# The first modulation computed by pairs of feature tiles, with five strips in flight and unused products between them

## The chip, the cores and the metric

The kernel runs on one core of one Trainium2 chip. TensorE (PE, with its weight load PEld) multiplies; VectorE (DVE) and ScalarE (ACT) do the elementwise work; GpSimd (POOL) does little here; SyncE (SP) issues the DMAs. The metric is the device time of one execution in microseconds (us). Lower is better.

## The reference, cut to what matters

Two blocks run one after the other. The change lies in the opening of layer 0 of the first one. With x of 256 tokens by 1024 features and a conditioning vector c:

```python
mod = silu(c) @ w_ada + b_ada
shift, scale, gate = split(mod, 3, axis=-1)
h = rmsnorm(x, norm_g) * (1.0 + scale) + shift
proj = h @ w_in
...
xbc = silu(causal_dwconv(xbc, conv_w, conv_b))
...
dt = softplus(dt_raw + dt_bias)
```

The 3072 columns of `mod` are 1024 of shift, 1024 of scale and 1024 of gate. Nothing of `proj` can be complete before all 1024 features of h are modulated, so before all of shift and scale are known. Rotary tables (sine and cosine of the positions) are used further on, by the retention heads.

## The kernel before

**Layout.** Features lie on partitions, as eight tiles of 128 features by 256 tokens; x is one buffer of 1 MB. A column block of 128 of `w_in` is a *strip*: its weights come as one 0.5 MB transfer `raw` (L491), ACT copies them, rounded, into `hi` (through the helper at L479), DVE writes the remainder `lo = raw - hi` (L506), and PE multiplies (`mm3`, L533 to L535) with three products for each feature tile: hi by h_hi, hi by h_lo, lo by h_hi. A strip is 8 x 3 = 24 products of 128x128 by 128x256 into one accumulator bank. `hi` and `lo` have three buffers each; strip 3 is one of a few named in `EXTRA` and uses two other buffers (`ret_o`, `fox_v`). The strips come in a fixed list; the first nine are four of the convolution's B and C part, one for dt and the gates' inputs, and then four of the convolution's xs part.

**The modulation.** `mod` comes in rounds of 512 columns. A round is 4 raw tiles of 0.5 MB, loaded as two transfers of 1 MB into two of four buffers (`yd`, `qk_ret`, `xs`, `xdt`, which other steps use later), so that two rounds are in flight. PE multiplies each half of a round in 16 small products with 32 columns of silu(c) (L718, on the trace 32 records, since each is two passes), ACT copies the sums (`ada_0s` to `ada_3s`), PE transposes them (L725) and DVE adds the bias (`mod`). Rounds 0 and 1 are the shift, rounds 2 and 3 the scale; `first_norm` takes them in the order 0, 2, 1, 3. After 0 and 2 feature tiles 0 to 3 of h can be made, after 1 and 3 tiles 4 to 7: for each tile ACT writes `h_hi`, DVE the modulated value (L472) and `h_lo` (L457).

**The norm.** Beside that ACT and DVE square and add x (`sq`, `acc`), PE sums over partitions (L635), DVE makes the reciprocal root in small steps (`rs13y`), PE spreads it over partitions (L644) and DVE multiplies x by it (`qk_fox`). Then come 8 products of 128x128 that spread silu(c) (`spread`, L783), whose results are used by the later rounds on VectorE.

**The strips behind it.** Strips 0, 1 and 2 start with what tiles 0 to 3 give; `BEHIND` holds their first products behind products of rounds 1 and 3. Each finished strip of B and C goes through `conv4`: ACT writes `cv_y` from the bank, DVE adds three shifted taps (`cv_y`, 255, 254 and 253 wide), ACT makes `cv_t`, DVE multiplies into `BC`. Strip 4 goes through `dtf` (`dtf_z`, the softplus `sp`, running sums). Banks of tag `mm` are three; the third tap frees one. Between them stand DVE's 16 steps and ACT's two lookups for the rotary tables (`rot_ang`, `rot_n`, `rot_r`, `rsin`, `rcos`; L831).

**Order.** Instructions on an engine run in the order that a scheduler gives them by priorities and by `issue_after` edges; an engine waits at the head of its queue.

## Time and profile before

| | us |
|---|---|
| median of 3 runs | 2198.2 |
| lowest, highest | 2197.14, 2200.11 |
| profiled execution, its own time | 2200.12 |
| its span, first to last instruction | 2198.4 |
| PE busy in the span | 2146.0 (98%) |
| DVE busy in the span | 1714.4 (78%) |
| ACT busy in the span | 1000.6 (46%) |

All the rest of the document reads one profiled execution. A row of the timeline gives the start of an instruction (or of a run of like ones, x n), its duration, what it is, output from inputs with partitions and elements, and in brackets how long the engine had been idle before it and what it then had waited for. A row of the windows gives for a stretch the busy time of each engine with its instruction count. Durations of neighbours overlap by about 0.1 us, since an engine starts the next before the last has drained; where costs are added, the distance between two starts is used.

### The profile page before, as it was taken

Reading aid. Unit: us, or ns where it says so; the run is one execution under the profiler, and the core shown is the slowest. Engines: PE = TensorE matmul, PEld = TensorE weight load, DVE = VectorE, ACT = ScalarE, POOL = GpSimd, SP = SyncE. Lnnn points to the kernel's source line nnn. Section 1 sums busy time; section 2 is a strip of 40 time slices with the busy share of each in tenths; the row PEclk is TensorE's granted clock in tenths of the full one; section 3 lists DMA queues with packets and bytes.
Section 4 is the critical chain, followed back from the end, with each engine's and each line's share of the span. In section 5 each row is a group of like instructions: output and inputs, shape, how many; then the busy total and the mean of one; then the engine's idle time right before and its main releaser. Section 6 shows DMA issues by size and latency. Waiting matters only on the chain. (4 is left out here: it accounts for less than half of the span.)

```text
span 2198.4 us, 38207 instructions
## 1 busy us (share of the span) xinstructions
PE 2146.0 (98%) x14481; PEld 1910.5 (87%) x14481; DVE 1714.4 (78%) x3551; ACT 1000.6 (46%) x1828; POOL 72.0 (3%) x657
## 2 busy tenths in 40 slices
PE   6999999999999999999999999999999999999999
PEld 5999989898877888888888888888887999999999
DVE  6986889798975999775476777766689977567877
ACT  4656555555455333432333443323355434445654
POOL 0000000001000000000000000000000000000000
PEclk9999999999999999999999999999999999999999
DMA  8665746567321144235443244453432453674665
GB/s 301 198 202 176 268 135 201 160 215 235 106 68 53 50 128 144 82 123 160 125 154 110 82 125 128 122 181 122 122 116 72 128 156 126 210 249 145 186 195 158
DMA packets 98264, 330.71 MB, mean 150 GB/s; under 512 B 10912, under 2 KB 14368, under 8 KB 97952
## 3 DMA queue, kind: packets, MB, share of 16 engines
q1 hardware_dynamic: 97632, 326.47, 47.0%
q8 instruction: 114, 1.87, 0.4%
q0 software_dynamic: 448, 1.81, 0.2%
q14 instruction: 70, 0.57, 0.1%
HBM read 325.08 MB, written 3.15 MB: 149 GB/s over the span
## 5 line engine op out<-in xcount | busy, mean ns | idle before, releaser
L479 ACT ACTIVATE hi<-raw 128x1024 fp32r<-128x1024 f32 (+3 forms) x494 | 492.0, 997 | 709.0 <-PE mm L534 440.0
L506 DVE TENSOR_TENSOR lo<-raw,hi 128x1024 fp32r<-128x1024 f32 (+3 forms) x494 | 565.0, 1144 | 231.0 <-ACT hi L479 228.3
L533 PE MATMUL mm<-h,hi 128*128 128x512 f32 (+1 forms) x1296 | 445.7, 345 | 3.4 <-ACT th L479 1.2
L535 PE MATMUL mm<-h,lo 128*128 128x512 f32 (+1 forms) x1296 | 442.0, 342 | 2.5 <-DVE lo L506 2.5
L534 PE MATMUL mm<-h,hi 128*128 128x512 f32 (+1 forms) x1296 | 442.1, 342 | 0.4 <-DVE h L475 0.4
L533 PEld LDWEIGHTS mm<-h,hi 128*128 128x128 f32 x1296 | 244.3, 189 | 33.7 <-ACT h L479 1.5
L535 PEld LDWEIGHTS mm<-h,lo 128*128 128x128 f32 x1296 | 244.8, 189 | 32.3 <-DVE lo L506 3.3
L534 PEld LDWEIGHTS mm<-h,hi 128*128 128x128 f32 x1296 | 244.7, 189 | 30.3 <-DVE h L475 0.8
L533 PE MATMUL mm<-hi,h 128*128 128x256 f32 x608 | 173.2, 285 | 0.8 <-ACT h L479 0.7
L534 PE MATMUL mm<-lo,h 128*128 128x256 f32 x608 | 171.8, 283 | 1.2 <-DVE lo L506 1.2
L535 PE MATMUL mm<-hi,h 128*128 128x256 f32 x608 | 172.2, 283 | 0.1
L533 PE MATMUL mm<-h_hi,hi 128*128 128x256 f32 x512 | 143.7, 282 | 4.0 <-ACT h_hi L479 2.3
L535 PE MATMUL mm<-h_hi,lo 128*128 128x256 f32 x512 | 143.4, 282 | 1.3 <-DVE lo L506 1.2
L534 PE MATMUL mm<-h_lo,hi 128*128 128x256 f32 x512 | 143.8, 282 | 0.7 <-DVE h_lo L457 0.5
L475 DVE SCALAR_TENSOR_TENSOR cv<-glu,vec,cv 128x512 f32<-128x512 f32 (+1 forms) x240 | 136.4, 615 | 2.5 <-ACT cv L479 2.4
L766 DVE SCALAR_TENSOR_TENSOR ada<-ada,cb 128x1024 f32<-128x1024 f32 x104 | 126.8, 1220 | 1.3 <-DMA ada<-aall 0.8
L533 PEld LDWEIGHTS mm<-hi,h 128*128 128x128 f32 x608 | 114.4, 188 | 2.7 <-ACT h L479 1.8
L534 PEld LDWEIGHTS mm<-lo,h 128*128 128x128 f32 x608 | 114.5, 188 | 2.1 <-DVE lo L506 1.4
L535 PEld LDWEIGHTS mm<-hi,h 128*128 128x128 f32 x608 | 114.6, 189 | 1.3 <-DVE h L475 0.9
L533 PEld LDWEIGHTS mm<-h_hi,hi 128*128 128x128 f32 x512 | 96.1, 188 | 5.1 <-ACT h_hi L479 2.7
L535 PEld LDWEIGHTS mm<-h_hi,lo 128*128 128x128 f32 x512 | 96.1, 188 | 2.1 <-DVE lo L506 1.9
L534 PEld LDWEIGHTS mm<-h_lo,hi 128*128 128x128 f32 x512 | 96.3, 188 | 1.6 <-DVE h_lo L457 1.1
(679 smaller groups left out, 4821.9 us busy)
## 6 DMA issues: line engine op xcount, KB each, us to landing
raw<-wall SPq DMA_DIRECT2D x400, 512.0 KB, 3.7
ada<-aall SPq DMA_DIRECT2D x120, 512.0 KB, 4.2
raw<-wall SPq DMA_DIRECT2D x32, 384.0 KB, 3.1
raw<-wall SPq DMA_DIRECT2D x32, 320.0 KB, 3.1
raw<-wall SPq DMA_DIRECT2D x32, 256.0 KB, 2.7
yd<-aall SPq DMA_DIRECT2D x2, 1024.0 KB, 10.3
qk_ret<-aall SPq DMA_DIRECT2D x2, 1024.0 KB, 11.3
xs<-aall SPq DMA_DIRECT2D x2, 1024.0 KB, 10.8
```

Of the source, the lines that this page charges most:

```text
L475: return self.nc.vector.scalar_tensor_tensor(out=out, in0=a, scalar=s, in1=b, op0=op0, op1=op1)
L479: return self.nc.scalar.activation(out, a, f, bias=bias, scale=scale, **kw)
L506: self.last_lo = self.nc.vector.tensor_tensor(lo[:, :w], raw[:, :w], hi[:, :w].bitcast(F32), op=ALU.subtract)
L533: mm(ps, ah, bh, start=first and n == 0, stop=False)
L534: mm(ps, ah, bl, start=False, stop=False)
L535: self.last_mm = mm(ps, al, bh, start=False, stop=last and n == len(A) - 1)
L766: nc.vector.scalar_tensor_tensor(out=out, in0=raw, scalar=1.0, in1=self.cb[which][i], op0=ALU.mult, op1=ALU.mult, accum_out=m[:, n:n + 1])
```

## The change

The rounds 0 to 3 are cut otherwise: round r now holds the 256 columns of shift and the 256 of scale of feature tiles 2r and 2r+1, so each round completes one pair of tiles. x and the second group of vectors are loaded ahead of the first round's weights. Five strips (`FIRST_STRIPS`) advance with the rounds: after round 1 all five multiply tiles 0 to 3 (60 products), after round 2 three of them tiles 4 and 5 (18), after round 3 the two others (`OWED`) catch up on tiles 4 and 5 (12) and all five take tiles 6 and 7 (30). Strip 4 also gets buffers of its own (`fox_k`, `fox_o`, its raw tile under the tag `ada`), and two strips use banks of the tag `aux`. `idle` adds products of the identity by itself, which nothing reads: 20 ahead of round 0's first half, and then after each first half, after each second half and after each transpose the numbers in `IDLE`, 69 in all. The `spread` moves from the norm to behind the third strip's first part. The constants' second group (801 KB), the fox mask, the small dt vector and the rotary tables are held behind the split of strip 6 or later, the tables with a low priority (`ROT_LATE`).

```diff
@@ -31,7 +31,7 @@
...
 ADA_STRIPS = [a + d * i for a, d, n in ADA_AT for i in range(n)]
-EXTRA = (3, 72, 244, 423)
+EXTRA = (3, 4, 72, 244, 423)
 FIRST_TAGS = ("yd", "qk_ret", "xs", "xdt")
@@ -49,8 +49,12 @@
...
 ZFIRST = 4
-SPREAD = 0
-BEHIND = ((1, 3), (3, 3), (3, 3))
+FIRST_STRIPS = 5
+IDLE = ((20, 4, 6), (6, 2, 10), (4, 2, 8), (1, 2, 1, 3))
+OWED = 3
+ROT_LATE = 260
 ADA_LATE = 300
@@ -172,18 +176,20 @@
-FIRST_ROUNDS = (0, 2, 1, 3)
+def _mixed(which, l, r):
+    return (which, l) == (1, 0) and r < 4
 def _ada_plan():
...
         for l in range(2):
-            order = FIRST_ROUNDS + (4, 5) if (name, l) == ("w_ada", 0) else range(rounds)
-            for r in order:
+            which = 1 if name == "w_ada" else 2
+            for r in range(rounds):
                 for q in range(4):
-                    if (1 if name == "w_ada" else 2, l, r) in ON_PE:
-                        s.append((name, l, _full(2, 256 * q), ((512 * r, 512),)))
+                    if (which, l, r) in ON_PE:
+                        cols = ((256 * r, 256), (1024 + 256 * r, 256)) if _mixed(which, l, r) else ((512 * r, 512),)
+                        s.append((name, l, _full(2, 256 * q), cols))
                     else:
@@ -487,10 +492,13 @@
...
         nm = f"{self.wpos}"
-        raw = self.wp.tile([P, 1024], F32, tag="raw", name="raw" + nm, bufs=RAW_BUFS)
+        early = self.wpos in EXTRA and self.wpos < FIRST_STRIPS
+        tag, bufs = ("ada", 2) if early else ("raw", RAW_BUFS)
+        raw = self.wp.tile([P, 1024], F32, tag=tag, name="raw" + nm, bufs=bufs)
         self.nc.sync.dma_start(out=raw[:, :w], in_=self.wall[self.woff:self.woff + P * w].rearrange("(p w) -> p w", p=P))
         if self.wpos in EXTRA and self.wpos < N_PLAN1:
-            hi, lo = [self.bt([P, 1024], tag, FR, 1) for tag in ("ret_o", "fox_v")]
+            tags = ("fox_k", "fox_o") if self.wpos == 4 else ("ret_o", "fox_v")
+            hi, lo = [self.bt([P, 1024], tag, FR, 1) for tag in tags]
         elif self.wpos in EXTRA:
@@ -570,6 +578,12 @@
...
         return self.last_ada
+    def idle(self, n):
+        for _ in range(n):
+            mm = self.nc.tensor.matmul(self.scrap[:, :P], self.ident, self.ident, start=True, stop=True)
+        return mm
     def warm(self, behind, act, n):
@@ -587,12 +601,11 @@
...
             self.bg.popleft()()
-    def proj_f(self, name, act, T0, T, behind=None):
+    def proj_f(self, name, act, T0, T):
         w = self.strip(name)
         ps = self.mm_bank()
-        with self.tc.issue_after(behind.ins) if behind else nullcontext():
-            self.mm3(ps[:, :T], w, [(a[:, T0:T0 + T], b[:, T0:T0 + T]) for a, b in act])
+        self.mm3(ps[:, :T], w, [(a[:, T0:T0 + T], b[:, T0:T0 + T]) for a, b in act])
         return ps[:, :T]
@@ -717,17 +730,26 @@
...
                                           start=k == 0, stop=k == 7)
-            self.round_mm[which, l, r, q] = mm
+            if idle and q == 1:
+                with self.tc.issue_after(mm.ins):
+                    mm = idle(0)
+        if idle:
+            with self.tc.issue_after(mm.ins):
+                mm = idle(1)
         self.last_ada = mm
...
         pt = self.ps("tr")
-        nc.tensor.transpose(pt[:, :P], s, self.ident)
+        self.last_tr = nc.tensor.transpose(pt[:, :P], s, self.ident)
         def finish():
...
                 col = 0 if which == 1 else 1 + i
-                self.add(m[:, 4 * r:4 * r + 4], pt[:, col:P:32], b)
+                if _mixed(which, l, r):
+                    two = lambda a: a[:, 0:16].rearrange("p (a k) -> p a k", a=2)[:, :, 2 * r:2 * r + 2]
+                    self.add(two(m), pt[:, 0:P:32].rearrange("p (a k) -> p a k", a=2), two(self.v("b_ada0")))
+                else:
+                    self.add(m[:, 4 * r:4 * r + 4], pt[:, col:P:32], b)
         if later:
@@ -884,19 +906,18 @@
...
         if l == 0:
-            self.first_norm(rb, h)
+            first = self.first_norm(rb, h)
         else:
+            first = []
             mod = self.mods[1, l][0]
...
         for n in range(4):
-            behind = self.round_mm[(1, 0) + BEHIND[n]] if l == 0 and n < len(BEHIND) else None
-            self.conv4(l, self.proj_f("w_in", h, 0, T, behind), 8 + n, BC[:, n])
+            self.conv4(l, first.pop(0) if first else self.proj_f("w_in", h, 0, T), 8 + n, BC[:, n])
             self.pump()
-        ps = self.proj_f("w_in", h, 0, T)
+        ps = first.pop(0) if first else self.proj_f("w_in", h, 0, T)
         self.dtf(l, ps)
@@ -1020,31 +1041,73 @@
...
         g = self.v("norm_g0")
-        for half in range(2):
-            for r in FIRST_ROUNDS[2 * half:2 * half + 2]:
-                self.adaq.popleft()
-                if r != FIRST_ROUNDS[0]:
-                    self.ada_round(1, 0, r, self.ada_load(1, 0, r, self.first_tags()))
-                if r == FIRST_ROUNDS[SPREAD]:
-                    for f in self.spread(1, self.b1):
-                        f()
-            if half == 0:
-                for _ in range(3):
-                    self._fetch()
+        strips, pss = [], []
+        for r in range(4):
+            self.adaq.popleft()
+            if r:
+                idle = lambda i, r=r: self.idle(IDLE[r][i])
+                if r == 1:
+                    with self.tc.issue_after(self.last_mm.ins):
+                        self.ada_round(1, 0, r, self.ada_load(1, 0, r, self.first_tags()), idle=idle)
+                    for _ in range(FIRST_STRIPS):
+                        self._fetch()
+                    for n in range(FIRST_STRIPS):
+                        strips.append(self.strip("w_in", 0))
+                        pss.append((self.scrap if n == 0 else self.ps("mm" if n < 3 else "aux"))[:, :256])
+                    with self.tc.issue_after(self.last_tr.ins):
+                        self.last_mm = self.idle(IDLE[r][2])
+                    self.scrap = self.ps("aux")
+                else:
+                    with self.tc.issue_after(self.last_mm.ins):
+                        self.ada_round(1, 0, r, self.ada_load(1, 0, r, self.first_tags()), idle=idle)
             mod = self.mods[1, 0][0]
-            c = slice(4 * half, 4 * half + 4)
-            self.stt(a[:, c], mod[:, 8 + 4 * half:12 + 4 * half], 1.0, g[:, c], ALU.add, ALU.mult)
-            for k in range(4 * half, 4 * half + 4):
+            c = slice(2 * r, 2 * r + 2)
+            self.stt(a[:, c], mod[:, 8 + 2 * r:10 + 2 * r], 1.0, g[:, c], ALU.add, ALU.mult)
+            for k in range(2 * r, 2 * r + 2):
                 ak, sh = a[:, k:k + 1], mod[:, k:k + 1]
...
                 self.sub(h[k][1], xr[:, k], h[k][0].bitcast(F32))
+            if r:
+                ks = slice(0 if r == 1 else 2 * r, 2 * r + 2)
+                if r > 1:
+                    with self.tc.issue_after(self.last_tr.ins):
+                        self.last_mm = self.idle(IDLE[r][2])
+                groups = [(i, w, ps) for i, (w, ps) in enumerate(zip(strips, pss))]
+                if r == 3:
+                    for i, w, ps in self.owed:
+                        with self.tc.issue_after(self.last_tr.ins):
+                            self.mm3(ps, w[4:6], h[4:6], first=False, last=False)
+                    with self.tc.issue_after(self.last_mm.ins):
+                        self.last_mm = self.idle(IDLE[r][3])
+                for i, w, ps in groups[:OWED] if r == 2 else groups:
+                    with self.tc.issue_after(self.last_mm.ins):
+                        self.mm3(ps, w[ks], h[ks], first=r == 1, last=r == 3)
+                    if r == 1 and i == 2:
+                        with self.tc.issue_after(self.last_mm.ins):
+                            for f in self.spread(1, self.b1, "tr"):
+                                f()
+                self.owed = groups[OWED:]
+        for _ in range(2):
+            self._fetch()
         self.load_group(self.b1, 1, "cst")
+        self.start_ends = self.last_hi.ins, self.last_lo.ins
         self.idr = self.b1.tile([P, P], FR, tag="idr", name="idr", bufs=1)
...
         self.act(self.idr, self.ident, AF.Copy)
-        self.act(self.fmask, self.c("foxmask"), AF.Copy)
-        self.rotary_tables()
+        with self.behind_start():
+            self.act(self.fmask, self.c("foxmask"), AF.Copy)
+        with self.behind_start(), self.prio(ROT_LATE):
+            self.rotary_tables()
+        return pss
+    @contextmanager
+    def behind_start(self):
+        with self.tc.issue_after(self.start_ends[0]), self.tc.issue_after(self.start_ends[1]):
+            yield
     def first_tags(self):
@@ -1055,10 +1118,11 @@
...
         b = self.ncpool.tile([P, 4], F32, tag="dtf_b", name=f"dtf_b{l}")
-        self.mul(b[:, 0:1], self.v(f"dtf_b{l}"), sg)
-        self.act(b[:, 1:2], self.v(f"a_log{l}"), AF.Exp)
-        self.ts(b[:, 1:2], b[:, 1:2], -1.0, ALU.mult)
+        with self.behind_start():
+            self.mul(b[:, 0:1], self.v(f"dtf_b{l}"), sg)
+            self.act(b[:, 1:2], self.v(f"a_log{l}"), AF.Exp)
+            self.ts(b[:, 1:2], b[:, 1:2], -1.0, ALU.mult)
         z = self.bt([P, 256], "dtf_z", bufs=1)
@@ -1903,9 +1967,12 @@
...
                 self.ftag = -2
-                self.ada_round(1, 0, FIRST_ROUNDS[0], self.ada_load(1, 0, FIRST_ROUNDS[0], self.first_tags()))
                 nc.sync.dma_start(out=self.x1, in_=self.xT_d)
                 self.load_group(self.b1, 1, "vec")
+                self.scrap = self.ps("mm")
+                with tc.issue_after(self.idle(IDLE[0][0]).ins):
+                    self.ada_round(1, 0, 0, self.ada_load(1, 0, 0, self.first_tags()),
+                                   idle=lambda i: self.idle(IDLE[0][1 + i]))
                 for l in range(2):
```

What this does to the order shows at three places. On PE, at the program's start, the products of the rounds (L718 before, L731 after), the norm (L635 and L644; L648 and L657), the spread (L783) and the strips (L533 to L535; L541 to L543) stand in a row as follows. Before:

```order
L725 MATMUL tr_133<-cst_69,ada_0s 128x128
L718 MATMUL tr_213<-xs_209,cT 32x128
L635 MATMUL aux_162<-ones,acc_139 128x1 x2
L718 MATMUL tr_213<-xs_209,cT 32x128 x15
L644 MATMUL aux_181<-cst_69,rs13y 128x128 x2
L783 MATMUL aux_197<-cst_69,cT 128x128 x4
L783 MATMUL aux_203<-cst_69,cT 128x128 x4
L718 MATMUL tr_213<-xdt_211,cT 32x128 x16
L725 MATMUL tr_248<-cst_69,ada_2s 128x128
L718 MATMUL tr_286<-yd_282,cT 32x128 x16
L718 MATMUL tr_286<-qk_ret_284,cT 32x128 x16
L533 MATMUL mm_409<-h_hi_184,hi_253 128x256
```

After (L584 is the unused product):

```order
L584 MATMUL mm_96<-cst_69 128x128 x20
L731 MATMUL tr_122<-yd_117,cT 32x128
L648 MATMUL aux_193<-ones,acc_170 128x1 x2
L731 MATMUL tr_122<-yd_117,cT 32x128 x15
L584 MATMUL mm_96<-cst_69 128x128 x4
L657 MATMUL aux_212<-cst_69,rs14y 128x128 x2
L731 MATMUL tr_122<-qk_ret_119,cT 32x128 x16
L584 MATMUL mm_96<-cst_69 128x128 x6
L743 MATMUL tr_167<-cst_69,ada_0s 128x128
L731 MATMUL tr_238<-xs_234,cT 32x128 x16
L584 MATMUL mm_96<-cst_69 128x128 x6
L731 MATMUL tr_238<-xdt_236,cT 32x128 x16
```

The spread is gone from here; x's norm stands within the first round, whose second half follows its broadcast, and all of the second round comes ahead of the first strip.

On PE, later, around the third and fourth round, before (banks mm_409 and mm_448 are strips 0 and 1):

```order
L533 MATMUL mm_409<-h_hi_184,hi_253 128x256
L534 MATMUL mm_409<-h_lo_185,hi_253 128x256
L535 MATMUL mm_409<-h_hi_184,lo_254 128x256
L718 MATMUL tr_328<-xs_324,cT 32x128 x16
L718 MATMUL tr_328<-xdt_326,cT 32x128 x16
L533 MATMUL mm_448<-h_hi_184,hi_259 128x256
L534 MATMUL mm_448<-h_lo_185,hi_259 128x256
L535 MATMUL mm_448<-h_hi_184,lo_260 128x256
L533 MATMUL mm_448<-h_hi_184,hi_259 128x256
L725 MATMUL tr_363<-cst_69,ada_3s 128x128
L534 MATMUL mm_448<-h_lo_185,hi_259 128x256
L535 MATMUL mm_448<-h_hi_184,lo_260 128x256
```

After (aux_317 is strip 4, mm_96 strip 0):

```order
L542 MATMUL aux_317<-h_lo_216,fox_k_310 128x256
L543 MATMUL aux_317<-h_hi_215,fox_o_311 128x256
L731 MATMUL tr_413<-yd_409,cT 32x128 x16
L584 MATMUL aux_328<-cst_69 128x128 x4
L731 MATMUL tr_413<-qk_ret_411,cT 32x128 x16
L584 MATMUL aux_328<-cst_69 128x128 x2
L743 MATMUL tr_454<-cst_69,ada_2s 128x128
L584 MATMUL aux_328<-cst_69 128x128 x8
L541 MATMUL mm_96<-h_hi_215,hi_286 128x256
L542 MATMUL mm_96<-h_lo_216,hi_286 128x256
L543 MATMUL mm_96<-h_hi_215,lo_287 128x256
L541 MATMUL mm_96<-h_hi_215,hi_286 128x256
```

Before, products of strips 0 and 1 on tiles 0 to 3 stand between the rounds; after, the rounds stand behind all five strips' first parts, with unused products in between.

On DVE, behind the last tile of h, before (lo_484 is strip 4's, cv_y_434 strip 0's):

```order
L506 TENSOR_TENSOR fox_v_445<-raw_442,ret_o_444 128x1024
L472 TENSOR_SCALAR rot_n<-rot_ang 128x128
L475 SCALAR_TENSOR_TENSOR cv_y_434<-mm_409,vec_137,cv_y_434 128x255
L470 TENSOR_SCALAR rot_n<-rot_n 128x128
L475 SCALAR_TENSOR_TENSOR cv_y_434<-mm_409,vec_137,cv_y_434 128x254
L475 SCALAR_TENSOR_TENSOR rot_r<-rot_n,rot_ang 128x128
L475 SCALAR_TENSOR_TENSOR cv_y_434<-mm_409,vec_137,cv_y_434 128x253
L475 SCALAR_TENSOR_TENSOR rot_r<-rot_n,rot_r 128x128
L475 SCALAR_TENSOR_TENSOR cv_y_473<-mm_448,vec_137,cv_y_473 128x255
L475 SCALAR_TENSOR_TENSOR rot_r<-rot_n,rot_r 128x128
L475 SCALAR_TENSOR_TENSOR BC_408<-cv_t_435,cv_y_434 128x256
L472 TENSOR_SCALAR rot_r<-rot_r 128x128
```

After (lo_591 and lo_597 are those of strips 5 and 6, cv_y_630 and cv_y_638 strips 0 and 1):

```order
L462 TENSOR_TENSOR h_lo_216<-qk_fox_217,h_hi_215 128x256
L514 TENSOR_TENSOR lo_591<-raw_588,hi_590 128x1024
L514 TENSOR_TENSOR lo_597<-raw_594,hi_596 128x1024
L480 SCALAR_TENSOR_TENSOR cv_y_630<-mm_96,vec_94,cv_y_630 128x255
L480 SCALAR_TENSOR_TENSOR cv_y_638<-mm_314,vec_94,cv_y_638 128x255
L480 SCALAR_TENSOR_TENSOR cv_y_630<-mm_96,vec_94,cv_y_630 128x254
L480 SCALAR_TENSOR_TENSOR cv_y_638<-mm_314,vec_94,cv_y_638 128x254
L480 SCALAR_TENSOR_TENSOR cv_y_630<-mm_96,vec_94,cv_y_630 128x253
L480 SCALAR_TENSOR_TENSOR cv_y_638<-mm_314,vec_94,cv_y_638 128x253
L462 TENSOR_TENSOR dtf_b_662<-vec_94,cst_600 128x1
L480 SCALAR_TENSOR_TENSOR BC_629<-cv_t_631,cv_y_630 128x256
L475 TENSOR_SCALAR dtf_b_662<-dtf_b_662 128x1
```

The steps of the rotary tables are gone from between the taps; the splits of strips 3 and 4 stand ahead of the last tiles of h, and the splits of strips 5 and 6 ahead of all taps.

## Rows read from the trace of the kernel before

**Rows 1.** The page, busy time of each engine, share of the span, instructions

```profile
PE 2146.0 (98%) x14481; PEld 1910.5 (87%) x14481; DVE 1714.4 (78%) x3551; ACT 1000.6 (46%) x1828; POOL 72.0 (3%) x657
```

**Rows 2.** Windows: busy time by engine in stretches of the start, granted clock, DMA

```profile
core 0: us, PE busy (x) PEld busy (x) DVE busy (x) ACT busy (x) POOL busy (x), PEclk, DMA share, GB/s
0.00:7.00 7.00, 0.00 (x0) 0.00 (x0) 1.17 (x7) 1.81 (x3) 0.20 (x4) 1.00 0.69 222
...
60.00:70.00 10.00, 9.07 (x74) 8.54 (x74) 9.94 (x23) 5.68 (x10) 0.00 (x0) 1.00 0.42 112
...
90.00:100.00 10.00, 10.00 (x86) 9.14 (x86) 9.43 (x21) 5.52 (x11) 0.00 (x0) 1.00 0.54 171
```

**Rows 3.** Windows, one longer stretch behind it

```profile
100.00:150.00 50.00, 49.87 (x421) 46.94 (x421) 46.24 (x99) 27.23 (x50) 0.00 (x0) 1.00 0.60 188
```

**Rows 4.** Timeline of PE to 30 us: start, duration, instruction, wait before it

```profile
7.19 1.94 PE L718 MATMUL tr<-yd,cT 128*32 128x128 f32 x32 [7.19 <-DMA yd<-aall]
9.63 1.93 PE L718 MATMUL tr<-qk_ret,cT 128*32 128x128 f32 x32 [0.51 <-DMA qk_ret<-aall]
...
19.95 1.22 PE L644 MATMUL aux<-cst,rs13y 128*128 128x128 f32 x4 [0.56 <-DVE rs13y L475]
20.96 3.00 PE L783 MATMUL aux<-cst,cT 128*128 128x128 f32 x16
23.89 1.08 PE L718 MATMUL tr<-xdt,cT 128*32 128x128 f32 x32
...
26.37 1.08 PE L718 MATMUL tr<-yd,cT 128*32 128x128 f32 x32
27.45 1.08 PE L718 MATMUL tr<-qk_ret,cT 128*32 128x128 f32 x32
29.68 0.38 PE L533 MATMUL mm<-h_hi,hi 128*128 128x256 f32 x1 [1.15 <-ACT h_hi L479]
```

**Rows 5.** Timeline of ACT, the first step on x

```profile
12.17 0.42 ACT L479 ACTIVATE acc<-x 128x256 f32<-128x256 f32 x1 [0.26 <-DMA x<-xT]
```

**Rows 6.** Line L783 later on (record count, min/median/max ns, first and last start)

```profile
L783 PE MATMUL aux<-cst,cT x32: 275/275/377, 144.5 to 148.1; 128*128 128x128 f32 x32
```

**Rows 7.** Timeline of PE, products of the strips

```profile
41.05 0.28 PE L534 MATMUL mm<-h_lo,hi 128*128 128x256 f32 x1
41.17 0.28 PE L535 MATMUL mm<-h_hi,lo 128*128 128x256 f32 x1
...
49.47 0.28 PE L535 MATMUL mm<-h_hi,lo 128*128 128x256 f32 x1
51.19 0.36 PE L533 MATMUL mm<-h_hi,hi 128*128 128x256 f32 x1 [1.44 <-DVE cv_y L475]
...
62.52 0.39 PE L535 MATMUL mm<-h_hi,lo 128*128 128x256 f32 x1 [0.89 <-DVE lo L506]
```

**Rows 8.** Timeline of DVE, from the rotary tables to strip 8's split

```profile
41.16 0.93 DVE L472 TENSOR_SCALAR rot_n<-rot_ang 128x128 f32<-128x128 f32 x1
...
49.44 1.21 DVE L506 TENSOR_TENSOR lo<-raw,hi 128x1024 fp32r<-128x1024 f32 x1
50.57 0.87 DVE L475 SCALAR_TENSOR_TENSOR cv_y<-mm,vec,cv_y 128x253 f32<-128x253 f32 x2
51.35 1.22 DVE L506 TENSOR_TENSOR lo<-raw,hi 128x1024 fp32r<-128x1024 f32 x1
52.48 0.42 DVE L475 SCALAR_TENSOR_TENSOR BC<-cv_t,cv_y 128x256 f32<-128x256 f32 x1
...
56.25 1.76 DVE L819 RECIPROCAL sp<-sp 128x128 f32<-128x128 f32 x2
57.92 0.49 DVE L457 TENSOR_TENSOR cbm<-aux,cst 128x384 f32<-128x384 f32 x1
...
61.24 1.22 DVE L506 TENSOR_TENSOR lo<-raw,hi 128x1024 fp32r<-128x1024 f32 x1
```

**Rows 9.** Timeline of ACT, a table load for the rotary lookups

```profile
45.13 1.28 ACT L479 ACT_TABLE_LOAD   x1
```

11 lines of the change are left out of this document (5 added, 6 removed).

## The prediction

> **What bounds the kernel now.** The page comes first: PE is busy 98% of the span, DVE 78% [rows 1]. An edit can therefore only gain where PE still idles, and that is the opening, which is where this change lies. Next come the windows, to see how long the opening lasts: between 60 and 70 us PE is busy 9.07 of 10, while DVE is busy 9.94; from 90 to 100 us PE is busy all 10, and 49.87 of the next 50 [rows 2, 3]. So PE does not idle again for long after 63 us: whatever it is late (or early) there it keeps to the end, and the question of this case is how late PE is with the strip that it multiplies at 62.5 us. But rows 2 also show who leads there: DVE is saturated from 60 us on.
>
> The timeline of PE shows the opening itself. PE waits for the first weights until 7.19 us, does two half-rounds in 1.94 and 1.93 us, waits again, spreads the norm at 19.95, and multiplies the first strip at 29.68 us [rows 4]. After that product, which itself waited 1.15 us for the first tile of h, two gaps matter: 1.44 us before strip 5 at 51.19, whose bank a convolution tap (`cv_y`) on DVE had to free, and 0.89 us at 62.52, where the split (`lo`) of strip 8 came late from DVE [rows 7]. The timeline of DVE shows what stands ahead of that split: between strip 5's split at 49.44 and strip 8's at 61.24 lie 11.8 us [rows 8].
>
> **The change part by part.**
>
> *Loads.* x is issued where the first weights were, so it should land at about 7.2 instead of 12.17 us [rows 4, 5]. Between those two landings lie two others of 1 MB, so a transfer of 1 MB takes about (12.17 - 7.19)/2 = 2.5 us. The rounds' eight transfers then land at about 9.7, 12.2, 15 and 17.5 us, the five raw tiles of 0.5 MB by 24, and the last four at 26.5, 29, 31.5 and 34. PE, below, needs none of the last four sooner: no cost.
>
> *The norm.* From x's landing to the product that spreads it went 19.95 - 12.17 = 7.8 us, 0.5 of it because the sum over partitions ran at half speed; I take 7.3, from 7.2 to 14.5 us.
>
> *Speed of PE.* The same half-round takes 1.94 us at 7.19 and 1.08 us at 23.89, so PE stands at its lower level (1.2 GHz) early and at the higher (2.4 GHz) after the busy stretch that begins at 19.95 [rows 4]. The column of the granted clock says 1.00 from the first slice on [rows 2] and is no help. The 20 unused products can start when the identity's small transfer is in and fill the time to the first weights, so I take the higher level from then on. A spread or unused product is two records: 32 of them from 144.5 to 148.1 is 3.6/16 = 0.22 us for one at the higher level [rows 6], and 3.00/8 = 0.38 us at the changing one [rows 4]. What the Trainium skill says of this ("TensorE: Matmul & The Clock Gate", section "What's actually happening") is that "the default state is throttled, and activity releases the throttle". By that the 20 products pay at once and the sum below stands; but the trace speaks against it in one place, since the two half-rounds from 7.19 to 11.56 did not release it. That is the third rival.
>
> *To the first strip.* From 14.5: broadcast 0.45, half-round 1.08, 6 unused 1.33, transpose 0.25, half-round 1.08, 6 unused 1.33, half-round 1.08, 2 unused 0.45, transpose 0.25, 10 unused 2.2: 9.5 us, to 24.0. The strips start 5.7 us earlier than at 29.68.
>
> *First parts of five strips.* Products of a strip start 0.117 us apart (41.05 to 41.17 [rows 7]): 60 cost 7.0. Strip 0 must wait for the remainder of tile 3, since DVE now does the splits of strips 0 to 2 ahead of it (three of 1.13, from 49.44 to 50.57 [rows 8]): some 2.2. The spread, moved here, 8 x 0.22 = 1.8. To 35.0.
>
> *Round 2.* 2 x 1.08, unused 6 x 0.22 = 1.33, transpose 0.25, unused 8 x 0.22 = 1.8: 5.5. These unused products cover the copy and the chain transpose, bias, modulation, h_hi (about 1 us each), so only about 1 us of them is not wait anyway. Then 18 strip products 2.1: 42.6.
>
> *Round 3.* 2.16, 3 unused 0.67, transpose 0.25, 1 unused 0.2; 12 owed products 1.4; 3 unused 0.67: 48.0. Then strip 0's last six until 48.7 and all 30 until 51.5. Before, five strips were done shortly after 49.47 [rows 7], so the early start of 5.7 us is already gone at the end of the five: it went to rounds 2 and 3, which before ran with strip products beside them and now stand in the open, with 21 + 8 spread and unused products of 0.22 (6.4 us).
>
> *Strip 5.* Its `hi` needs a buffer of strip 0, free at 48.7; ACT's copy takes 1.05, so DVE starts its split at about 49.8. The order now puts the splits of strips 5 and 6 ahead of all taps: two of 1.13, then taps of strips 0 and 1 by turns, 0.39 each (50.57 to 51.35 for two); the fifth frees a bank at 54.0. PE starts strip 5 at about 54.1 against 51.19: 2.9 us later.
>
> *Strip 8, the term that sets the end.* What DVE has between strip 5's and strip 8's split: 3 splits 3.4; 15 taps 5.85 (before, eight of those of strips 0 to 2 were done by then); 4 products into `BC` at 0.34, 1.4; the softplus up to there, with its two reciprocals of 1.67 together (56.25 to 57.92), 4.3; two masks `cbm` 0.9; small ones 0.2. Sum 16.1 against 11.8. From 49.8 that is 65.9 instead of 61.24: **4.7 us**. The reason is plain: all five strips end together at 51, so their convolutions start together, while DVE sits idle between the rounds; before, strips 0 to 2 ended earlier and their taps lay in the 41 to 49 us that now have little work.
>
> *Rotary tables.* Sixteen steps, the longest 0.93 [rows 8], the others about 0.15, 3.3 us together, and ACT's table loads of 1.28 [rows 9] leave the opening and come back behind strip 13. There DVE is busy 9.43 of 10, and later 46.24 of 50 [rows 2, 3]: it costs from 0 (taken up by DVE's 3.8 us of rest) to 3.3 (DVE leads all the way). I take 0.8, nearer to the rest. ACT is at 5.5 of 10 and hides its part.
>
> *Sum.* 4.7 + 0.8 = **5.5 us later**. The rest of the program is in the same order. The profiled execution was 2200.1 us and would be 2205.6; its time stands 1.9 above the median of the runs, so against the median 2198.2 + 5.5 = 2203.7.
>
> **The rivals.**
>
> *The early start carries through (faster).* Strips start 5.7 us earlier. If the unused products and the waits of rounds 2 and 3 lie within waits that are there anyway, and strip 0's last product frees its `hi` early, DVE's backlog starts early too. It decides at strip 5's split on DVE: the backlog is 4.3 us longer than before, so that split must start before 49.44 - 4.3 = 45.1 for strip 8 to be on time. At the full gain the time is some 6 us less, 2192; the middle is 2195. For it: PE idles 1.15 us at 29.68, and the tables' 3.3 us have left DVE. Against it: 6.4 us of products that compute nothing new stand on PE's queue behind 26 us.
>
> *DVE's rest eats it (no change).* The backlog of 4.7 us is on DVE, and PE waits for it only as long as the strips' splits have no lead. The splits of strips 3 and 4 and the tables are out of the way, and 3.8 us of rest on DVE follow in rows 3. Then the lateness shrinks to 1 to 4 us: 2199 to 2202.
>
> *The unused products don't raise the clock (slower).* If PE stays at 1.2 GHz until about 23 us as it did before, three half-rounds cost 0.86 more each and 24 unused products about 0.2 more, in part under the wait for x: about 5 us more, 2209.
>
> **How the numbers follow.** The forecast has a chance of 0.49, no change 0.30, the faster case 0.13, the clock 0.08. The predicted time is 2203.7. A measurement of this kernel can tell about 0.2%, 4.4 us, from no change; that puts the forecast and the clock above, the second rival within, the first below: faster 0.13, same 0.30, slower 0.57. The range: 2196 leaves out the better half of the faster case, 2209 the worse half of the clock and the tables' upper bound of 3.3 with a later strip 8. The forecast's own range is 2202 to 2207.
>
> **What would show it.** Right: half-rounds of 1.08 us from the first on; the first strip product near 24 us; round 2 of the modulation behind five first parts near 35; strip 5 near 54, waiting for `cv_y`; DVE idle for several microseconds between 29 and 38 and between 40 and 46; a wait of 1 to 2 us for strip 8's split near 66. Wrong: half-rounds of 1.9 us at the start (the clock); strip 5's split on DVE before 45 us (the faster case); PE and DVE at strip 14 or later as far on as before, in spite of a late strip 8 (DVE's rest).

## The result, and the profile of the changed kernel

The changed kernel takes 2211.89 us (median of 4 runs, 2207.52 to 2214.10) against 2198.75 us (4 runs, 2197.14 to 2200.11): ratio 1.0058, 95% interval 1.0040 to 1.0075. It is slower by 13 us. The sign is as forecast; the size is not, since the forecast was 5.5 us and the range ended at 2209. Five more runs beside other kernels gave 2210.85 (2208.89 to 2211.69), ratio 1.0053 (1.0039 to 1.0066). The profiled execution took 2211.34 us, with a span of 2209.6 against 2198.4: 11.2 us to explain.

The page, busy time by engine; [rows 1] is its counterpart:

```profile
PE 2162.8 (98%) x14619; PEld 1928.3 (87%) x14619; DVE 1714.2 (78%) x3553; ACT 1001.7 (45%) x1828; POOL 72.0 (3%) x657
```

PE has 138 more records, the unused products, and 16.8 us more busy time. DVE's work is the same.

The windows of the changed kernel: stretch, its length, busy time and count of PE, PEld, DVE, ACT and POOL, granted clock, DMA share, GB/s. They answer to [rows 2]:

```profile
51.20:60.00 8.80, 6.16 (x44) 5.80 (x43) 7.11 (x15) 5.88 (x12) 1.90 (x2) 0.90 0.35 119
60.00:70.00 10.00, 9.54 (x72) 9.22 (x70) 8.71 (x23) 5.59 (x10) 0.00 (x0) 0.92 0.17 55
70.00:80.00 10.00, 8.16 (x53) 7.75 (x53) 8.70 (x20) 4.38 (x9) 0.00 (x0) 0.83 0.38 105
```

The last of them in the kernel before:

```profile
70.00:80.00 10.00, 10.00 (x87) 9.84 (x86) 9.94 (x18) 6.65 (x12) 0.00 (x0) 1.00 0.75 222
```

Before, PE was busy 10.00 of 10 from 70 to 80 us; now 8.16, and the granted clock, which was 1.00, is 0.83. Two things are wrong in this stretch: PE idles, and it is at half speed for a part of it.

The timeline of PE, by its landmarks; [rows 4, 7] are the counterparts:

```profile
3.18 6.56 PE L584 MATMUL mm<-cst 128*128 128x128 f32 x40 [3.18 <-DMA cst<-cst]
...
13.52 1.79 PE L584 MATMUL mm<-cst 128*128 128x128 f32 x8
...
16.16 1.60 PE L731 MATMUL tr<-qk_ret,cT 128*32 128x128 f32 x32
...
25.74 0.37 PE L541 MATMUL mm<-h_hi,hi 128*128 128x256 f32 x1
...
37.10 1.08 PE L731 MATMUL tr<-yd,cT 128*32 128x128 f32 x32
...
45.69 1.08 PE L731 MATMUL tr<-xs,cT 128*32 128x128 f32 x32
...
51.07 0.36 PE L541 MATMUL mm<-h_hi,hi 128*128 128x256 f32 x1
...
54.82 0.28 PE L543 MATMUL aux<-h_hi,fox_o 128*128 128x256 f32 x1
57.74 0.36 PE L541 MATMUL mm<-h_hi,hi 128*128 128x256 f32 x1 [2.64 <-DVE cv_y L480]
...
70.62 0.39 PE L541 MATMUL mm<-h_hi,hi 128*128 128x256 f32 x1 [1.08 <-DVE cv_y L480]
72.08 0.58 PE L543 MATMUL mm<-h_hi,lo 128*128 128x256 f32 x1 [0.97 <-DVE lo L514]
```

The first strip starts at 25.74, 3.9 us earlier than before; the last product of the five strips starts at 54.82 instead of 49.47; strip 5 starts at 57.74 instead of 51.19, and the product on strip 8's split at 72.08 instead of 62.52. So the opening loses 9.6 us from a start that was 3.9 us ahead.

The timeline of DVE; [rows 8] is the counterpart:

```profile
41.10 0.16 DVE L462 TENSOR_TENSOR mod<-tr,vec 128x4 f32<-128x4 f32 x1 [9.67 <-PE tr L743]
...
49.03 0.16 DVE L462 TENSOR_TENSOR mod<-tr,vec 128x4 f32<-128x4 f32 x1 [5.24 <-PE tr L743]
...
53.28 2.36 DVE L514 TENSOR_TENSOR lo<-raw,hi 128x1024 fp32r<-128x1024 f32 x2 [1.57 <-ACT hi L484]
55.56 2.42 DVE L480 SCALAR_TENSOR_TENSOR cv_y<-mm,vec,cv_y 128x255 f32<-128x255 f32 x6
...
63.66 0.29 DVE L475 TENSOR_SCALAR sp<-sp 128x256 f32<-128x256 f32 x1 [1.27 <-ACT sp L484]
...
70.81 1.22 DVE L514 TENSOR_TENSOR lo<-raw,hi 128x1024 fp32r<-128x1024 f32 x1
```

DVE stands idle for 9.67 and 5.24 us, each time for a transpose of rounds 2 and 3, and then has 17.5 us of work from strip 5's split (53.28) to strip 8's (70.81), against 11.8 before.

### The profile page after: what moved, and what is told of

The parts are those of the page before. It is cut to its first block, busy times and chain, and to the rows that moved or that the text cites. A ratio compares the mean times of both kernels' runs of the same rounds, so it can differ in the third digit from the quotient of the medians.

```text
span 2209.6 us, 38487 instructions
## 1 busy us (share of the span) xinstructions
PE 2162.8 (98%) x14619; PEld 1928.3 (87%) x14619; DVE 1714.2 (78%) x3553; ACT 1001.7 (45%) x1828; POOL 72.0 (3%) x657
## 5 line engine op out<-in xcount | busy, mean ns | idle before, releaser
L541 PE MATMUL mm<-h,hi 128*128 128x512 f32 (+1 forms) x1296 | 445.5, 344 | 3.3 <-ACT th L484 1.2
L543 PE MATMUL mm<-h,lo 128*128 128x512 f32 (+1 forms) x1296 | 441.4, 341 | 2.6 <-DVE lo L514 2.6
L541 PEld LDWEIGHTS mm<-h,hi 128*128 128x128 f32 x1296 | 243.9, 188 | 33.7 <-ACT h L484 1.5
L543 PEld LDWEIGHTS mm<-h,lo 128*128 128x128 f32 x1296 | 244.4, 189 | 32.4 <-DVE lo L514 3.3
L541 PE MATMUL mm<-hi,h 128*128 128x256 f32 x608 | 173.5, 286 | 0.8 <-ACT h L484 0.7
L543 PE MATMUL mm<-hi,h 128*128 128x256 f32 x608 | 172.7, 284 | 0.1
L541 PE MATMUL mm<-h_hi,hi 128*128 128x256 f32 x504 | 143.2, 285 | 4.8 <-DVE cv_y L480 3.7
L543 PE MATMUL mm<-h_hi,lo 128*128 128x256 f32 x504 | 142.5, 284 | 1.8 <-DVE lo L514 1.8
L541 PEld LDWEIGHTS mm<-hi,h 128*128 128x128 f32 x608 | 115.0, 189 | 2.6 <-ACT h L484 1.8
L543 PEld LDWEIGHTS mm<-hi,h 128*128 128x128 f32 x608 | 115.4, 190 | 1.0 <-DVE h L480 0.7
L541 PEld LDWEIGHTS mm<-h_hi,hi 128*128 128x128 f32 x504 | 96.1, 191 | 5.4 <-issue 2.8
L543 PEld LDWEIGHTS mm<-h_hi,lo 128*128 128x128 f32 x504 | 96.0, 191 | 2.5 <-DVE lo L514 2.5
## 6 DMA issues: line engine op xcount, KB each, us to landing
yd<-aall SPq DMA_DIRECT2D x2, 1024.0 KB, 10.9
```

Source lines behind the costliest of these rows:

```text
L541: mm(ps, ah, bh, start=first and n == 0, stop=False)
L543: self.last_mm = mm(ps, al, bh, start=False, stop=last and n == len(A) - 1)
```

## The experiments

Each run has one profiled execution. A diff is against the changed kernel where nothing else is said; dots stand for lines that are not shown. Two theories. **S, the schedule:** rounds 2 and 3 stand behind all first parts, the unused products lengthen them, the five strips end late and together, and DVE's backlog passes that on to strips 5 and 8. **C, the clock:** TensorE's level falls, or is held up by the unused products, and that makes or saves the time.

### Without the unused products of rounds 2 and 3 (a_noidle23)

```diff
-IDLE = ((20, 4, 6), (6, 2, 10), (4, 2, 8), (1, 2, 1, 3))
+IDLE = ((20, 4, 6), (6, 2, 10), (0, 0, 0), (0, 0, 0, 0))
...
```

> The changed kernel without the 21 unused products of rounds 2 and 3; those ahead of the first strip stay. Theory S (the schedule: rounds 2 and 3 stand in the open behind all first parts, and the unused products only lengthen that): they take 5.0 us of PE from start to start in the trace of the changed kernel, some 2.7 of it under waits that are there anyway (copy, transpose, modulation), so strip 5 starts about 2.3 us earlier than at 57.74 and the time is about 2209.6. Theory C (the clock: the products hold TensorE at its higher level): without them the level falls within rounds 2 or 3, half-rounds take 1.6 to 1.9 us, and the time is 2212 or more.

2208.36 us (6 runs, 2205.84 to 2214.26), ratio 1.0043 (1.0030 to 1.0056). Timeline of PE in round 2, and at strip 5:

```profile
35.72 1.08 PE L732 MATMUL tr<-yd,cT 128*32 128x128 f32 x32
36.62 1.06 PE L732 MATMUL tr<-qk_ret,cT 128*32 128x128 f32 x32
38.13 0.33 PE L744 MATMUL tr<-cst,ada_2s 128*128 128x128 f32 x1 [0.46 <-ACT ada_2s L484]
39.55 0.39 PE L541 MATMUL mm<-h_hi,hi 128*128 128x256 f32 x1 [1.08 <-ACT h_hi L484]
...
54.56 0.36 PE L541 MATMUL mm<-h_hi,hi 128*128 128x256 f32 x1 [2.64 <-DVE cv_y L480]
```

Round 2 takes 3.8 us to its first strip product (35.72 to 39.55) instead of 5.5 (37.10 to 42.61), with half-rounds at full speed and waits of 0.46 and 1.08 us in place of the products: the level doesn't fall there without the products either. Theory S is right on the mechanism. On the time the interval overlaps that of the changed kernel; 3 us less is likely, not certain. Behind the same gap of 2.64 us ahead of strip 5 the level did not fall in this execution:

```profile
54.56:64.00 9.44, 9.44 (x77) 9.33 (x78) 9.35 (x24) 6.59 (x14) 0.00 (x0) 1.00 0.33 102
```

### Without any unused product (a_noidle)

```diff
-IDLE = ((20, 4, 6), (6, 2, 10), (4, 2, 8), (1, 2, 1, 3))
+IDLE = ((0, 0, 0), (0, 0, 0), (0, 0, 0), (0, 0, 0, 0))
...
-                with tc.issue_after(self.idle(IDLE[0][0]).ins):
+                with nullcontext():
```

> The changed kernel without any of the 69 unused products. Theory S: what rounds 2 and 3 give back is as in the run without their 21; at the start the half-rounds run at 1.94 us as in the kernel before, half of that under the waits for x and the norm, so the first strip starts between 25 and 27 us and the time is 2209 to 2212. Theory C: the low level reaches into the first strips (0.21 us from product to product) and comes back in rounds 2 and 3: 2214 or more.

2208.90 us (5 runs, 2207.69 to 2211.70), ratio 1.0042 (1.0029 to 1.0055). Timeline of PE:

```profile
15.70 1.94 PE L732 MATMUL tr<-qk_ret,cT 128*32 128x128 f32 x32
...
18.44 1.49 PE L732 MATMUL tr<-xs,cT 128*32 128x128 f32 x32
19.75 1.05 PE L732 MATMUL tr<-xdt,cT 128*32 128x128 f32 x32
...
22.22 0.39 PE L541 MATMUL mm<-h_hi,hi 128*128 128x256 f32 x1 [0.62 <-ACT hi L484]
```

Windows of the same run:

```profile
24.00:32.00 8.00, 5.82 (x29) 5.41 (x28) 5.43 (x7) 3.27 (x4) 0.00 (x0) 0.63 1.03 409
40.00:46.00 6.00, 4.12 (x18) 3.53 (x19) 1.91 (x6) 1.15 (x3) 0.00 (x0) 0.77 0.30 117
```

Both theories missed the start: the level rises within the third half-round anyway, and the first strip starts at 22.22 us, earlier than with the products. Theory C is right on what follows: the granted clock is 0.63 from 24 to 32 and 0.77 from 40 to 46, and all that was won at the start and by the shorter rounds is lost there (strip 5 starts at 58.04). On the time it is wrong: 2208.90 is at the lower end of what theory S said, and far from 2214. All 69 unused products together bring nothing: without them the time is, if anything, 2 to 3 us less.

### Two more stretches of unused products, to hold the level (a_keepclock)

```diff
+            if l == 0 and n == 1:
+                self.scrap = self.ps("aux")
+                with self.tc.issue_after(self.last_mm.ins):
+                    self.last_mm = self.idle(12)
...
+        with self.tc.issue_after(self.last_mm.ins):
+            self.idle(12)
```

> The changed kernel with 12 more unused products behind strip 4 (where PE idles 2.64 us before strip 5) and 12 behind strip 7 (where it idles 1.08 and 0.97 us around strip 8's start). Theory C: the two falls of the granted clock, at 58.3 and at about 72 us, don't come; the first costs little because PE waits for a tap again at 70.6, the second is 3.4 us at half speed, so the time is about 1.5 to 2 us less, 2210. Theory S: DVE leads up to 80 us in any case, and the time stays within 0.7 of 2211.9. If the products are in the way it is up to 1.5 more.

2209.35 us (5 runs, 2206.37 to 2210.29), ratio 1.0038 (1.0026 to 1.0050). Windows of the changed kernel where the level falls:

```profile
13.00:17.00 4.00, 4.00 (x50) 3.53 (x42) 2.35 (x13) 0.00 (x0) 0.00 (x0) 0.61 1.02 410
...
58.00:62.00 4.00, 4.00 (x23) 4.00 (x23) 3.91 (x11) 1.97 (x6) 0.00 (x0) 0.57 0.53 174
...
70.00:76.00 6.00, 4.42 (x23) 4.21 (x24) 6.00 (x14) 1.15 (x3) 0.00 (x0) 0.72 0.45 102
```

The same windows in this run:

```profile
13.00:17.00 4.00, 3.67 (x54) 3.16 (x52) 2.95 (x14) 0.28 (x1) 0.00 (x0) 1.00 1.02 409
...
58.00:62.00 4.00, 4.00 (x35) 3.97 (x34) 4.00 (x12) 2.86 (x6) 0.00 (x0) 1.00 0.47 142
...
70.00:76.00 6.00, 5.56 (x47) 5.16 (x45) 5.94 (x15) 2.87 (x5) 0.00 (x0) 1.00 0.58 178
```

Both later falls are gone (the first one, at 13 us, shows in no other trace of the changed kernel and its variants). Timeline of DVE in this run, splits of strips 5 and 8:

```profile
51.71 2.36 DVE L514 TENSOR_TENSOR lo<-raw,hi 128x1024 fp32r<-128x1024 f32 x2 [1.57 <-ACT hi L484]
...
67.81 1.22 DVE L514 TENSOR_TENSOR lo<-raw,hi 128x1024 fp32r<-128x1024 f32 x1
```

From split 5 to split 8 DVE now takes 16.1 us, instead of 17.5: with PE at full speed the softplus no longer waits 1.27 us for ACT. The span is 2205.0, 6.6 us over the kernel before, where the changed kernel was 11.2 over. Product by product, counted from the end of both traces, it is 4.3 us ahead of the changed kernel at 80 us and 4.6 at the end. So in this pair of executions the falls of the opening are 4.3 of the 11.2 us, and the schedule is the larger rest. By the times of all runs the share is smaller and less certain: the median is 10.1 us over that of the kernel before beside it, where the changed kernel is 12.4 and 13.1 over, so 2 to 3 us, and the intervals of the ratios overlap. Theory C has its part; theory S has the larger one.

### The rotary tables back where they were (a_rot)

```diff
-        with self.behind_start(), self.prio(ROT_LATE):
-            self.rotary_tables()
+        self.rotary_tables()
```

> The changed kernel with the rotary tables where they were before, right behind the last tiles of h and not held or late. Theory S: 16 steps of DVE (3.3 us) and two table loads of ACT (1.28 each) come back ahead of strip 5's bank, of which 1.6 us fall into DVE's wait for strip 5's hi at 51.7: strip 5 some 1.5 us later, and about 1 us less behind strip 13: 2211.5 to 2213. If the tables' late place is what costs (DVE leading from 80 to 100 us), 2209 to 2210.

2212.85 us (5 runs, 2208.87 to 2216.83), ratio 1.0058 (1.0046 to 1.0070): as theory S said. Strip 5, timeline of PE:

```profile
59.14 0.36 PE L541 MATMUL mm<-h_hi,hi 128*128 128x256 f32 x1 [3.86 <-DVE cv_y L480]
```

It starts 1.4 us later than in the changed kernel, but this execution did not have the fall of the level at 72 us: from 75 to 150 us the two are equally late, within 0.2 us. Behind 153 us this run is 1.5 us ahead, and later more (the wait is shown under v3). Over all runs the tables' old place gains nothing; it is not what the change lost on.

### The same, once more (a_same)

> The changed kernel once more, unaltered, beside the three others, for its scatter from run to run. Theory C': runs differ by how often the granted clock falls (the mean granted clock goes from 0.994 to 0.997 as the time goes from 2214 to 2207.5), so the median is 2209 to 2213 and the scatter 3 to 6 us, against 3 us of the kernel before.

(C' is theory C read over runs.) 2210.85 us. The scatter was 2.8 us here and 6.6 in the four runs of the result. Strip 5 started at 57.42, with the same gap of 2.64 us.

### Rounds as soon as their weights are there, strips one after the other (v2)

```diff
+            elif r > 1:
+                with self.tc.issue_after((self.last_mm if r == 2 else self.last_tr).ins):
+                    self.ada_round(1, 0, r, self.ada_load(1, 0, r, self.first_tags()),
+                                   idle=lambda i, r=r: part(r + 1, slice(0, 4), True, False) if i else None)
...
+        self.last_mm = self.last_tr
+        for f in self.spread(1, self.b1, "tr"):
+            with self.tc.issue_after(self.last_mm.ins):
+                f()
+        for i in range(FIRST_STRIPS):
+            with self.tc.issue_after(self.last_mm.ins):
+                part(i, slice(4, 8), False, True)
```

`part` is a strip's products on some of the tiles: the first parts of strips 3 and 4 stand where the unused products stood. Of the 69 unused products 21 go, and not 41 as the text below has it: 48 stay, and PE has 42 records fewer (14577 against 14619), two for each.

> The changed kernel up to the first parts of strips 0 to 2; then the rounds as soon as their weights are there (about 27 to 34 us), with the first parts of strips 3 and 4 in the holes instead of unused products, the spread behind round 3, and then strips 0 to 4 finished one after the other on tiles 4 to 7. 41 of the 69 unused products go with it, the 20 + 10 + 18 at the start stay. Theory S (the loss comes from rounds 2 and 3 standing in the open behind all first parts, so that five strips end together at 54.9 us): round 3 ends at about 38, strip 0 at about 41.5, strip 4 at about 47, DVE's taps start as early as before, strip 5 starts between 48 and 51, and the time is 2197 to 2201, about that of the kernel before. Theory C (the clock and the late tables make the loss): the time stays at 2206 or more.

2200.69 us (11 runs, 2198.77 to 2204.15), ratio 1.0011 (1.0002 to 1.0020): 10 to 11 of the 12 to 13 us are back; the last 2 are not. Timeline of PE, half-round of round 2, last transpose, strip 5:

```profile
32.65 1.08 PE L732 MATMUL tr<-yd,cT 128*32 128x128 f32 x32
...
39.67 0.27 PE L744 MATMUL tr<-cst,ada_3s 128*128 128x128 f32 x1
...
48.73 0.28 PE L541 MATMUL mm<-h_hi,hi 128*128 128x256 f32 x1
```

Timeline of DVE, splits of strips 5 and 8:

```profile
44.24 1.22 DVE L514 TENSOR_TENSOR lo<-raw,hi 128x1024 fp32r<-128x1024 f32 x1 [1.57 <-ACT hi L484]
...
60.34 1.22 DVE L514 TENSOR_TENSOR lo<-raw,hi 128x1024 fp32r<-128x1024 f32 x1
```

The last round is done 9 us earlier (transpose at 39.67 instead of 48.68), strip 5 starts at 48.73 with no wait, 2.5 us ahead of the kernel before, and strip 8's split starts at 60.34 instead of 61.24. Theory S named the loss. Of the 2.5 us that v2 is ahead at strip 5, 0.9 are left at strip 8's split, since DVE sets that. Behind it the level fell in this execution, and at 73 us v2 is 0.8 us behind the kernel before:

```profile
62.00:65.40 3.40, 3.40 (x18) 3.40 (x18) 3.40 (x8) 0.00 (x0) 0.00 (x0) 0.50 0.64 177
```

### The same, but the strips end together (v2_pairs)

The diff is against v2:

```diff
-        for i in range(FIRST_STRIPS):
-            with self.tc.issue_after(self.last_mm.ins):
-                part(i, slice(4, 8), False, True)
+        for q in (4, 6):
+            for i in range(FIRST_STRIPS):
+                with self.tc.issue_after(self.last_mm.ins):
+                    part(i, slice(q, q + 2), False, q == 6)
```

> The run v2 with one thing put back: behind the last round all five strips first take tiles 4 and 5, then all take tiles 6 and 7, so that they end within 3.5 us of each other as in the changed kernel. PE's work is the same. If the ending together is what loads DVE (theory S's second half): strip 4 still ends at about 47.5, but strip 0 at about 45 instead of 41.5, strip 5's hi and split follow 2.5 to 3 us later than in v2 (47 instead of 44.24), strip 8's split at 62.5 to 63.5 instead of 60.34, and the time is 2 to 3 us above v2. If only the place of the rounds counts: within 0.7 of v2.

2203.86 us (10 runs, 2201.97 to 2206.69), ratio 1.0021 (1.0012 to 1.0031): 3.2 us over v2, or 2.6 when each is taken against the kernel before beside it (4.9 and 2.3 over). Timelines, strip 5 on PE, then the splits of strips 5 and 8 on DVE:

```profile
49.91 0.36 PE L541 MATMUL mm<-h_hi,hi 128*128 128x256 f32 x1 [2.64 <-DVE cv_y L480]
```

```profile
45.45 2.36 DVE L514 TENSOR_TENSOR lo<-raw,hi 128x1024 fp32r<-128x1024 f32 x2 [4.32 <-ACT hi L484]
...
62.74 1.22 DVE L514 TENSOR_TENSOR lo<-raw,hi 128x1024 fp32r<-128x1024 f32 x1
```

With the same work on PE the gap of 2.64 us ahead of strip 5 is back, and strip 8's split comes 2.4 us later. Behind the gap the level fell here too (granted clock 0.50 from 51.4 to 54.8 us), so a part of the price can be the level's. The ending together has a price of its own, 2.6 to 3.2 us, and the place of the rounds, with the 21 unused products and the spread that moved with it, accounts for the other 7 to 8. Those three were not taken apart further than by a_noidle23.

### Two taps left out (a_notaps)

```diff
-        for s in (1, 2, 3):
+        for s in (1,) if l == 0 and n >= 8 else (1, 2, 3):
```

> The changed kernel without two of the three convolution taps of layer 0's strips 0 to 3 (8 steps of DVE of 0.39, 3.1 us left out of the computation). Theory S (DVE's backlog behind 53 us sets strips 5 and 8): strip 5 starts about 1.5 us earlier (four fewer steps ahead of its bank), the split of strip 8 about 3.1 us earlier, the gap around 70 to 72 us shrinks and with it the fall of the clock: 2206.5 to 2209. If PE's own order and the clock set the time there: within 0.7 of the changed kernel.

2204.72 us (5 runs, 2203.09 to 2209.96). Timelines, strip 5 on PE and strip 8's split on DVE:

```profile
56.27 0.38 PE L541 MATMUL mm<-h_hi,hi 128*128 128x256 f32 x1 [0.99 <-DVE cv_y L480]
```

```profile
66.71 1.22 DVE L514 TENSOR_TENSOR lo<-raw,hi 128x1024 fp32r<-128x1024 f32 x1
```

3.1 us of DVE's work taken away bring strip 8's split 4.1 us forward, and the time 6 to 7 us down, more than was expected. With a gap of 0.99 instead of 2.64 us ahead of strip 5 the level did not fall behind it in the profiled execution; that this is the rest of the gain is likely, and not shown. DVE sets the end of the opening.

### What the kernel before lacks (b_start, b_xonly, b_early)

The kernel before with x loaded first: with 20 unused products at the start (b_start), without (b_xonly), and without but with the raw tiles of strips 1 and 2 behind rounds 1 and 3 (b_early). The diff of the last against the kernel before; b_xonly has its last part alone:

```diff
                     self.ada_round(1, 0, r, self.ada_load(1, 0, r, self.first_tags()))
+                    self._fetch()
...
-            if half == 0:
-                for _ in range(3):
-                    self._fetch()
...
-                self.ada_round(1, 0, FIRST_ROUNDS[0], self.ada_load(1, 0, FIRST_ROUNDS[0], self.first_tags()))
                 nc.sync.dma_start(out=self.x1, in_=self.xT_d)
                 self.load_group(self.b1, 1, "vec")
+                self.ada_round(1, 0, FIRST_ROUNDS[0], self.ada_load(1, 0, FIRST_ROUNDS[0], self.first_tags()))
```

> The kernel before with only x loaded ahead of the first weights and 20 unused products at the start. The norm is spread at about 15 instead of 19.95 us and half-rounds take 1.08. The first strip starts behind round 1's two half-rounds, whose weights land at about 27, so at 28 to 29 instead of 29.68, and round 3 still ends at about 35.5 when its weights are there: strip 5 within 0.5 us of 51.19 and the time within 1 of the kernel before. If the early part itself were what the kernel before lacks, it would gain 3 us or more.

> The kernel before with x loaded first and nothing else: b_start without its 20 unused products. Theory S: x ahead is what moved strip 5 by 1.2 us in b_start, since the level fell again in the waits for round 1's weights anyway: within 0.7 of b_start, 2196.5 to 2198. Theory C (the products at the start count): as the kernel before, 2198 to 2200.

> The kernel before with x loaded first, no unused product, and the raw tiles of strips 1 and 2 loaded behind rounds 1 and 3 instead of ahead of them. Theory S (before, the opening is bound by the last round's weights, 32.5 us, and then by DVE): the last weights land about 2.5 us earlier, h is complete that much earlier, strip 5 starts at 48.5 to 50 instead of 51.19 and the time is 2 to 3 us under that of the kernel before. If DVE alone sets the opening's end (taps, splits), it is within 1.3 of it, as with x first alone.

| | median us (runs) | ratio, 95% interval | strip 5 starts |
|---|---|---|---|
| b_start | 2197.42 (11) | 0.9994 (0.9986 to 1.0003) | 49.98 |
| b_xonly | 2197.42 (11) | 0.9992 (0.9983 to 1.0000) | 49.73 |
| b_early | 2196.75 (11) | 0.9988 (0.9979 to 0.9997) | 52.62 |

b_start and b_xonly are alike: x first brings 1.2 to 1.5 us at strip 5, the unused products nothing. b_early is the only version whose interval lies under 1, by a hair; its interval and that of b_xonly overlap almost whole. The reason is not the one expected: its strip 5 starts later than before, because PE waits 2.50 us at strip 3 for the rotary steps:

```profile
44.77 0.41 PE L533 MATMUL mm<-h_hi,ret_o 128*128 128x256 f32 x1 [2.50 <-DVE rot_r L472]
...
52.62 0.36 PE L533 MATMUL mm<-h_hi,hi 128*128 128x256 f32 x1 [0.43 <-DVE cv_y L475]
```

Its profiled execution is 1.4 us behind the kernel before through the opening and 1.8 us ahead at the end. Of the 3.2 us between, 2.4 come at about 1207 and 1627 us, where the level of the kernel before fell (granted clock 0.83 from 1205 to 1215 and from 1625 to 1635 us) and that of b_early did not (1.00 in both). So in this pair of executions the gain is not the opening's; why the median is lower is not explained here.

### The tables in DVE's rest (v3)

The diff is against v2:

```diff
+                self.load_group(self.b1, 1, "cst")
...
-        self.load_group(self.b1, 1, "cst")
...
-        with self.behind_start(), self.prio(ROT_LATE):
+        with self.prio(-150):
             self.rotary_tables()
```

> The run v2 with the constants' second group (801 KB) loaded ahead of the third round's weights and the rotary tables not held, so that their 16 steps fall into DVE's rest behind strip 4's split (31 to 36 us in v2). Theory S (what v2 still loses is DVE's work, of which the tables are 3.3 us behind strip 13): the third round's weights come 2 us later, at about 29, still ahead of PE, which gets to them at 32.6; about 1 us less than v2: 2198 to 2200. If the load delays the rounds after all, or the tables' two lookups on ACT stand in the way of h_hi: 2201 to 2204.

2201.34 us (11 runs, 2197.87 to 2205.65), ratio 1.0008 (0.9999 to 1.0017): not to be told from v2. In the profiled executions v3 was 0.5 us behind v2 up to 138 us and 1.4 ahead from 145 us on. What differs there is one more wait of PE, which the changed kernel and v2 have, both with late tables,

```profile
153.36 0.38 PE L541 MATMUL mm<-hi,h_hi 128*128 128x256 f32 x1 [1.08 <-ACT hi L484]
```

(1.36 us at 142.89 in v2) and which neither v3 nor a_rot has. It stands 55 us behind the two table loads of the changed kernel (91.87 and 97.63 us), and how late tables lead to it is not shown. Over 11 runs it doesn't come out of the scatter.

## Why the prediction was right and wrong

The sign and the main mechanism were right: the rounds in the open with unused products between them, the five strips ending together, and a backlog on DVE that sets strips 5 and 8. The size was wrong by more than a factor of two: 13.1 against 5.5 us. Two steps failed, the level of TensorE and the term of strip 8.

| | forecast | changed kernel | a_keepclock |
|---|---|---|---|
| first strip | 24.0 | 25.74 | 24.19 |
| round 2 begins | 35.0 | 37.10 | 35.55 |
| round 3 begins | 42.6 | 45.69 | 44.13 |
| strip 0's last six | 48.0 | 51.07 | 49.50 |
| split of strip 5 | 49.8 | 53.28 | 51.71 |
| strip 5 starts | 54.1 | 57.74 | 56.17 |
| split of strip 8 | 65.9 | 70.81 | 67.81 |
| from split 5 to split 8 | 16.1 | 17.5 | 16.1 |

**The first step that failed is in "Speed of PE": "I take the higher level from then on".** In the execution without a fall in the opening (a_keepclock) the steps hold to 0.2 us at the first strip and to 1.9 us at strip 8, and DVE's sum of 16.1 us is met exactly, as it is in v2 (44.24 to 60.34). In the changed kernel the level fell at 13.9 us (8 records of unused products in 1.79 us, a half-round in 1.60), and again at 58.3 and about 72 us, behind the gaps of 2.64 us and of 1.08 and 0.97 us which the change itself makes. At strip 8's split that is 3.0 us (70.81 against 67.81); of the time it is 2 to 3 us by the medians and 4.6 by the pair of traces. Those gaps were forecast, as "PE starts strip 5 at about 54.1" and "a wait of 1 to 2 us for strip 8's split"; what PE does after such a gap was not priced. The rows of before gave the price: 1.08 against 1.94 us for the same half-round [rows 4]. They did not show the fall: PE's gap of 1.44 us [rows 7] was followed by no fall before. The third rival looked for a low level only up to the first strips; two of the three falls came behind the five strips. The sentence of the Trainium skill that was quoted from "TensorE: Matmul & The Clock Gate", section "What's actually happening", calls the throttled state the default. These rows agree with that, in so far as the level fell behind gaps in TensorE's work; it did not fall behind each of them (a_noidle23).

**The second is the term of strip 8, 4.7 us, which was mis-sized** even with the level held: 67.81 - 61.24 = 6.6 us. The missing 1.9 us lie ahead of strip 5's split: the 18 products of round 2 took 3.1 instead of 2.1 us (42.61 to 45.69), since they wait for the h_lo of tiles 4 and 5 on DVE, and by the table some 0.4 us each lie in the first parts and between strip 0's last six and the split, 0.2 at the first strip.

**The tables' 0.8 us** stand for DVE's work from 80 to 150 us. There the lateness went from 11.5 to 12.0 us in the profiled execution, and at 153 us it rose by another 1.5, with the wait shown under v3; that this is the tables' is not shown. Moving them back costs 1.4 us at strip 5, and no version shows them as a loss. With the level held the medians are 10.1 us apart and the profiled executions 6.6; what makes up the difference between these two is open.

**That of round 2's unused products "only about 1 us of them is not wait anyway"** nearly held: 1.7 us of round 2 came back without them. That at the start they would bring the first strip forward did not hold: without any it started at 22.22.

**The rivals.** The faster case needed strip 5's split before 45.1; it came at 53.28, and v2, where it came at 44.24, was about as fast as the kernel before, as that decision point says. DVE's rest did not eat the lateness: between products of the same rank, counted from the end of both traces, the changed kernel was 10.9 us late at 75 us, 12.0 at 113 and 13.5 at 155. Further on it changes by 1 to 1.5 us at a time, where the level fell in one of the two executions and not in the other, to 11.2 at the end.
